# S5 recurrence of a hybrid diffusion step: sixteen lockstep chunk steps replaced by scan instructions on rotated states

## The chip, the cores and the metric

One core of a Trainium2 chip runs the whole program. The metric is the device time of one launch in microseconds, the median of the runs shown. Lower is better.

## The reference, cut to what matters

Two layers of a diffusion backbone work on 512 latent and 128 context tokens with 1024 channels. In each layer one projection feeds three mixers: a Hyena long convolution, a bidirectional S5 state space layer and a gated DeltaNet. The change lies in S5. It has 64 groups of 16 channels, each with 64 complex diagonal states per direction:

```python
lam_bar = jnp.exp(lam * step)
b_bar = ((lam_bar - 1.0) / lam)[..., None] * lax.complex(b_re, b_im)
bu = jnp.einsum('gph,blgh->blgp', b_bar, seq.astype(jnp.complex64))
bu = bu.at[:, 0].add(lam_bar * init)
_, xs = lax.associative_scan(_lin_combine, (a, bu), axis=1)   # x_t = lam_bar x_(t-1) + bu_t
finals.append(xs[:, -1])
yd = einsum('ghp,blgp->blgh', c_re, xs.real) - einsum('ghp,blgp->blgh', c_im, xs.imag)
```

It is run for both directions, for the latent tokens from cached states and for the context tokens from zero. The final context states are an output too.

## The kernel before

The residual stream lies transposed, channels on partitions and the 640 tokens along the free axis. Projections are products of split operands: a weight tile of 128x512 is loaded (`wr`), cast to `wh` on ACT (L69), its rest `wl` is formed on DVE or GpSimd (L70), and TensorE adds three products into `pj` or `pg` (L91). The order of the instructions on each engine isn't written by hand. The framework's scheduler makes it when the program is built, from the order in which the code is traced and from its own cost model; on the chip every engine then takes its instructions strictly in that order.

A layer has three parts: S5 and Hyena together, the DeltaNet, the merge. In the first, `run` takes turns between the generator `s5_core` and the generator `hyena`, one column tile (128 channels) each, eight times. The projections of the merge gates (`gates`, tile `pg`) are traced behind them and are drawn forward where TensorE would have nothing else. In layer 0 the modulation vectors (`mod_rest`, weights `in_wmod`, L286) are too.

For a column tile S5 works on 8 groups, with 64 states forward on the lower 64 partitions and 64 backward on the upper ones. The tokens are taken in 80 chunks of 8 (64 latent, 16 context):

- `s5_in` projects the tile, sends it through DRAM (`us`, then `U` with the 8 tokens of a chunk on partitions), builds the matrices `M2` on DVE and GpSimd (L824 to L829), and multiplies (L839): `X` holds what each chunk adds to the state. ACT moves it out of the accumulator (L841).
- `s5_scan` runs the recurrence over the chunks. The 80 chunks are five segments of 16, side by side. For each of 16 steps DVE does five small instructions (L884 to L888), and ACT copies the state that enters each chunk into `X`, once per direction (L895):

```python
nc.vector.tensor_tensor(out, z, bc(T["LR"]...), op=ALU.mult)
nc.vector.tensor_tensor(W, z[:, :, ::-1, :], bc(T["L2"]...), op=ALU.mult)
nc.vector.tensor_tensor(out, out, W, op=ALU.add)
for h, x in zip((lo, hi), add):
    nc.vector.tensor_tensor(out[h], out[h], x, op=ALU.add)
```

  Then the states that enter the later segments are chained (tile `C`) and their effect is added with the powers 0 to 15 of the chunk step, `FR` and `FI` (L912 to L916). GpSimd builds these powers by doubling in 24 small instructions (L865 to L871), and ACT adds a negated copy (L872).
- `s5_out` builds the read-out matrices `M3` (L949 to L954), the kernel of the convolution inside a chunk (`K`, through DRAM into `M1`), and multiplies (L981 to L983). In L981 and L982 the moving operand is `X[:, :, r, gi]`, whose neighbours along the chunks are 16 values apart.

`s5_core` traces `s5_in(i + 1)` and `s5_scan(i + 1)` ahead of `s5_out(i)`; `X` has two buffers.

Of the kernel before, what the change touches and what calls it, by code (L numbers as in the profile page):

```python
# [56 lines left out]
class Net:  # L57
# [242 lines left out]
    def mod_rest(self, l, p):  # L300
        """gate of layer l and all of layer l + 1"""
# [26 lines left out]
    def rstd_cols(self, p):  # L328
        """1/rms per token, tokens on partitions: [128, 5]"""
# [59 lines left out]
            # hidden layer of the filters: high parts above the low ones  # L389
# [12 lines left out]
    def hy_first(self, l, i, p):  # L402
        """channels 128 i .. 128 i + 127: spectra of the first order, factors of x1"""
# [10 lines left out]
    def hy_second(self, l, i, p, st):  # L414
        """spectra of the second order, factors of the output"""
# [11 lines left out]
    def hy_order1(self, l, i, p, st):  # L427
# [4 lines left out]
        # inverse, times x1, folded for the second order  # L432
# [78 lines left out]
    def filters(self, p, l, i, o, dec):  # L511
        """spectra (without the 1/norm) of order o for channel tile i"""
        nc, a, D, Dc = self.nc, self.a, self.D, self.Dc
        cs = slice(i * 128, i * 128 + 128)
        # forward + backward | forward - backward | forward columns, twice; high and low parts
# [19 lines left out]
        # even / odd parts of the two-sided filter, time tiles 0..127, 128..255 and their mirrors  # L535
# [3 lines left out]
        for t in range(2):  # L539
# [6 lines left out]
            # |fwd| + |bwd| = max(|fwd + bwd|, |fwd - bwd|)  # L546
# [59 lines left out]
        # slots 0: frequency 0 for Re, L for Im, each with half the weight of the others; even tile 1: L / 2  # L606
# [7 lines left out]
    def hy_in(self, p, l, t, rn, tag):  # L614
        """column tile -> conv -> folded, transposed: [time, 2, e | o, 128], context [time, 128]"""
# [229 lines left out]
    def s5_scan(self, l, ct, p, T):  # L845
# [44 lines left out]
        for s in range(16):  # L890
# [3 lines left out]
            for h, xv in zip((lo, hi), xs):  # L894
                nc.scalar.copy(xv, S[h])  # L895
# [768 lines left out]
```

## Time and profile before

| | |
|---|---|
| median of 3 runs | 3792.77 us (3789.83 to 3797.14) |
| span of the profiled execution | 3792.6 us |
| PE, PEld busy | 3401.0 us (90%), 3246.1 us (86%) |
| DVE, POOL, ACT busy | 2607.9 us (69%), 1692.8 us (45%), 1521.2 us (40%) |
| mean granted TensorE clock | 0.941 |

PE is TensorE's matmuls, PEld its weight loads, DVE VectorE, ACT ScalarE, POOL GpSimd. The profiled execution lies 0.2 us from the median, so its span stands for the time. The part of S5 and Hyena fills about 100 to 1000 us for layer 0 and 2000 to 2900 us for layer 1. The profile's chain of waits reaches back only to about 2979 us, behind both, so it says nothing on this part; the reading rests on the views that follow: stretches of time, waits, groups of instructions and single instructions.

### The profile page before, as it was taken

What the parts mean: (1) busy time and instruction counts of PE and PEld (TensorE: products, weight loads), DVE (VectorE), ACT (ScalarE), POOL (GpSimd) and SP (SyncE); (2) the same over time, 40 slices, a digit from 0 to 9 for tenths busy, and PEclk for the clock granted to TensorE, in tenths of its full rate; (3) what the DMA queues carried; (4) which work ended last, traced back from release to release, by engine and by line L of the source; (5) the groups of instructions that cost most, each with busy time, mean ns of one, the idle gap of its engine ahead of it and who ended that gap; (6) DMA issues with size and microseconds to landing.
All of it is one profiled execution on the core that took longest, in us unless ns stands there. A gap on an engine that the chain in (4) does not pass through costs nothing. (4 is left out here: it accounts for less than half of the span.)

```text
span 3792.6 us, 70255 instructions
## 1 busy us (share of the span) xinstructions
PE 3401.0 (90%) x25850; PEld 3246.1 (86%) x25850; DVE 2607.9 (69%) x6113; ACT 1521.2 (40%) x3519; POOL 1692.8 (45%) x2083
## 2 busy tenths in 40 slices
PE   6898988888989898899978899899899898798998
PEld 5788977788989888899977889898889898798998
DVE  6988788889237874643749788878883278776354
ACT  4533333333244555443334333333332445555422
POOL 4656555555344444301226565666654454351010
PEclk8899999999989999899989999999999899899999
DMA  6322233432231212543632222222222312224352
GB/s 226 113 75 67 75 94 103 119 97 58 79 86 63 71 60 71 175 141 111 197 104 77 73 65 73 75 81 72 72 61 73 96 63 78 61 92 140 126 176 89
DMA packets 310615, 362.89 MB, mean 96 GB/s; under 512 B 86814, under 2 KB 190270, under 8 KB 310016
## 3 DMA queue, kind: packets, MB, share of 16 engines
q1 hardware_dynamic: 305368, 357.75, 31.0%
q8 instruction: 204, 3.34, 0.4%
q10 hardware_dynamic: 4904, 0.66, 0.1%
q14 instruction: 139, 1.14, 0.1%
HBM read 291.74 MB, written 66.54 MB: 94 GB/s over the span
## 5 line engine op out<-in xcount | busy, mean ns | idle before, releaser
L91 PE MATMUL pj<-hh,wh 128*128 128x320 f32 x2048 | 670.7, 328 | 77.5 <-ACT wh L69 32.4
L91 PE MATMUL pj<-hl,wh 128*128 128x320 f32 x2048 | 662.0, 323 | 2.4 <-DVE hl L70 2.4
L91 PE MATMUL pj<-hh,wl 128*128 128x320 f32 x2048 | 660.0, 324 | 2.8 <-POOL wl L70 1.5
L69 ACT CAST wh<-wr 128x512 fp32r<-128x512 f32 x608 | 375.0, 618 | 598.4 <-PE pj L91 396.9
L70 POOL TENSOR_TENSOR wl<-wr,wh 128x512 fp32r<-128x512 f32 x288 | 382.4, 1331 | 517.0 <-ACT wh L69 466.9
L91 PEld LDWEIGHTS pj<-hh,wh 128*128 128x128 f32 x2048 | 404.3, 197 | 89.7 <-ACT wh L69 33.7
L91 PE MATMUL pg<-hh,wh 128*128 128x320 f32 x1280 | 416.6, 326 | 14.1 <-ACT wh L69 10.2
L91 PE MATMUL pg<-hl,wh 128*128 128x320 f32 x1280 | 412.8, 323 | 0.0
L70 DVE TENSOR_TENSOR wl<-wr,wh 128x512 fp32r<-128x512 f32 x320 | 244.1, 764 | 244.5 <-ACT wh L69 242.1
L91 PE MATMUL pg<-hh,wl 128*128 128x320 f32 x1280 | 409.9, 324 | 1.6 <-POOL wl L70 1.6
L91 PEld LDWEIGHTS pj<-hl,wh 128*128 128x128 f32 x2048 | 403.2, 197 | 6.5 <-DVE hl L70 5.3
L91 PEld LDWEIGHTS pj<-hh,wl 128*128 128x128 f32 x2048 | 402.4, 197 | 5.9 <-POOL wl L70 2.8
L91 PE MATMUL pj<-yh,wh 128*128 128x320 f32 x1024 | 316.8, 311 | 3.6 <-ACT yh L69 2.4
L91 PE MATMUL pj<-yl,wh 128*128 128x320 f32 x1024 | 317.4, 311 | 2.4 <-DVE yl L70 2.3
L91 PE MATMUL pj<-yh,wl 128*128 128x320 f32 x1024 | 316.4, 310 | 0.0
L895 ACT COPY X<-Z 64x80 f32<-64x80 f32 x512 | 131.1, 256 | 386.7 <-DVE Z L888 380.1
L91 PEld LDWEIGHTS pg<-hh,wh 128*128 128x128 f32 x1280 | 252.1, 197 | 18.9 <-ACT wh L69 11.3
L91 PEld LDWEIGHTS pg<-hh,wl 128*128 128x128 f32 x1280 | 249.1, 196 | 4.1 <-POOL wl L70 2.7
L91 PEld LDWEIGHTS pg<-hl,wh 128*128 128x128 f32 x1280 | 251.7, 197 | 0.7 <-issue 0.4
L888 DVE TENSOR_TENSOR Z<-Z,X 64x80 f32<-64x80 f32 x512 | 209.0, 408 | 13.7 <-ACT X L841 1.1
L91 PEld LDWEIGHTS pj<-yh,wh 128*128 128x128 f32 x1024 | 192.5, 189 | 4.9 <-ACT yh L69 3.2
L91 PEld LDWEIGHTS pj<-yl,wh 128*128 128x128 f32 x1024 | 192.8, 188 | 4.2 <-DVE yl L70 4.2
(513 smaller groups left out, 8757.1 us busy)
## 6 DMA issues: line engine op xcount, KB each, us to landing
wr<-in_wt SPq DMA_DIRECT2D x608, 256.0 KB, 2.7
gt<-gst SPq DMA_DIRECT2D x160, 160.0 KB, 2.0
gt<-gt SPq DMA_DIRECT2D x64, 320.0 KB, 3.3
wr<-in_wmod SPq DMA_DIRECT2D x64, 256.0 KB, 3.1
Pm<-gcd SPq DMA_DIRECT2D x32, 320.0 KB, 11.2
wm<-in_wmod SPq DMA_DIRECT2D x4, 2048.0 KB, 18.6
M<-ks SPq DMA_DIRECT2D x256, 32.0 KB, 1.8
xd<-x SPq DMA_DIRECT2D x16, 320.0 KB, 4.3
```

The lines of the kernel that those rows point to most:

```text
L69: self.nc.scalar.copy(h, src)
L70: (eng or self.nc.vector).tensor_tensor(l, src, h.bitcast(F32), op=ALU.subtract)
L91: ins = self.nc.tensor.matmul(o, w[:, k, :m], x[:, kh * 4 + k, s], start=kh == 0 and k == 0 and i == 0, stop=kh == 1 and k == 3 and i == 2)
L888: nc.vector.tensor_tensor(out[h], out[h], x, op=ALU.add)
L895: nc.scalar.copy(xv, S[h])
```

## The change

The step of a state over one chunk is a complex number of length `r8` and angle `theta`. Chunk states are turned back by their own angle (multiplied by e to the minus i theta c, with c the chunk's place), so that the recurrence has the real factor `r8`; then one scan instruction per real or imaginary part and direction does the whole recurrence, and the states are turned forward again. The columns of a group are now 83: 64 latent, 16 context, and places for entering states and a zero factor in `A` that stops the recurrence between segments and groups. The powers of the rotation, `E`, are built for each column tile on GpSimd by seven doublings, each of which takes its factor from two small ACT instructions. `E` and `A` have one buffer, `R` and `X` too; `X` now has its chunks side by side in memory. `s5_core` traces `s5_scan(i)`, then `s5_in(i + 1)`, then `s5_out(i)`. `s5_tables` computes the tables for this instead of those for the segments. The removed code is that of the kernel above.

```diff
@@ s5_core
+        E = cp.tile([128, 2, 8, 83], F32, name="E")
+        nc.gpsimd.memset(E[:, 0, :, 0:1], 1.0)
+        nc.gpsimd.memset(E[:, 1, :, 0:1], 0.0)
+        A = cp.tile([128, 8, 83], F32, name="A")
+        nc.gpsimd.memset(A, 0.0)
         self.s5_in(l, 0, p, T)
-        st = self.s5_scan(l, 0, p, T)
         for i in range(8):
-            now = st
+            now = self.s5_scan(l, i, p, T)
             if i < 7:
                 self.s5_in(l, i + 1, p, T)
-                st = self.s5_scan(l, i + 1, p, T)
             self.s5_out(l, i, p, T, *now)
+    def s5_turns(self, ct, p, T):
+        nc, E, A = self.nc, T["E"], T["A"]
+        gq = slice(8 * ct, 8 * ct + 8)
+        nc.scalar.copy(E[:, :, :, 1], T["V"][:, :, gq])
+        for x, n in ((slice(1, 65), 64), (slice(66, 82), 16)):
+            nc.scalar.copy(A[:, :, x], bc(T["r8"][:, gq].unsqueeze(2), [128, 8, n]))
+        e = 1
+        while e < 82:
+            n = min(e, 82 - e)
+            s, d = slice(1, 1 + n), slice(e + 1, e + 1 + n)
+            sh = [128, 2, 8, n]
+            m = p.tile([128, 2, 8, 1], F32, name="em", bufs=2)
+            nc.scalar.mul(m[:, 0], E[:, 1, :, e:e + 1], -1.0)
+            nc.scalar.copy(m[:, 1], E[:, 1, :, e:e + 1])
+            t = p.tile([128, 2, 8, 32], F32, name="et", tag="W5")[:, :, :, 0:n]
+            nc.gpsimd.tensor_tensor(E[:, 0:2, :, d], E[:, 0:2, :, s], bc(E[:, 0:1, :, e:e + 1], sh), op=ALU.mult)
+            nc.gpsimd.tensor_tensor(t, E[:, ::-1, :, s], bc(m, sh), op=ALU.mult)
+            nc.gpsimd.tensor_tensor(E[:, 0:2, :, d], E[:, 0:2, :, d], t, op=ALU.add)
+            e *= 2
@@ s5_in
-            nc.scalar.mul(T2[i][hi], src[hi, 0:8, gq], sg)
+        g.tensor_tensor(T2[hi, 0], pr, vr, op=ALU.mult)
...
-                nc.scalar.copy(X[:, :, r, ls].rearrange("p j g -> p g j"),
-                               pi.rearrange("p (g c) -> p g c", g=4)[:, :, 0:80])
+                nc.scalar.copy(R[:, r, ls, 1:83], pi.rearrange("p (g c) -> p g c", g=4)[:, :, 0:82])
+        nc.scalar.copy(R[:, :, :, 0:66:65], T["si"][:, :, gq, :])
@@ s5_scan
+        self.s5_turns(ct, p, T)
+        X = p.tile([128, 2, H, 83], F32, name="X5")
+        W = p.tile([128, H, 83], F32, name="W5")
+        re, im = E[:, 0], E[:, 1]
+        def turn(z, sg):
+            for r in range(2):
+                nc.vector.tensor_tensor(X[:, r], z[:, r], re, op=ALU.mult)
+                nc.vector.tensor_tensor(W, z[:, 1 - r], im, op=ALU.mult)
+                nc.vector.tensor_tensor(X[:, r], X[:, r], W, op=ALU.add if (r == 0) == (sg < 0) else ALU.subtract)
+        turn(R, -1)
+        for r in range(2):
+            z, b = [y[:, r].rearrange("p g c -> p (g c)") for y in (R, X)]
+            nc.vector.tensor_tensor_scan(z[lo], af[lo], b[lo], 0.0, op0=ALU.mult, op1=ALU.add)
+            nc.vector.tensor_tensor_scan(z[hi, n - 3::-1], af[hi, n - 1:1:-1], b[hi, n - 1:1:-1], 0.0,
+                                         op0=ALU.mult, op1=ALU.add)
+        turn(R, 1)
+        for h, s in ((lo, 81), (hi, 64)):
+            for r in range(2):
+                nc.scalar.mul(fs[h, :, r], X[h, r, :, s], -1.0 if r else 1.0)
@@ s5_out
-                nc.tensor.matmul(o, M3[:, 0, g, 1:9, :], X[:, :, 0, gi], start=True, stop=False)
+                nc.tensor.matmul(o, M3[:, 0, g, 1:9, :], X[:, 0, gi, 0:82], start=True, stop=False)
...
-            nc.scalar.copy(y[:, 320 * st:320 * st + 320], py[:, :320])
+            nc.scalar.copy(v[:, :, 0:64], o[:, :, 0:64])
+            nc.scalar.copy(v[:, :, 64:80], o[:, :, 65:81])
```

The scheduler makes a new order of the whole program. Three pieces of it, each from a column tile in the middle of layer 0, show what the prediction speaks of. The numbers behind the names are buffers; the brackets name the engines whose work an instruction waits for. First, DVE's queue before, in the middle of the recurrence. L667, L668 and L635 belong to Hyena.

```order
L886 TENSOR_TENSOR Z_4922<-Z_4922,W_4923 128x80 [waits DVE_49]
L888 TENSOR_TENSOR Z_4922<-Z_4922,X_4795 64x80 [waits DVE_49]
L888 TENSOR_TENSOR Z_4922<-Z_4922,X_4795 64x80
L667 TENSOR_TENSOR p1_5507<-pb_5498,KP_4471 128x512 [waits PE_49]
L884 TENSOR_TENSOR Z_4931<-Z_4922,LR_597 128x80 [waits DVE_49,Activation_49]
L885 TENSOR_TENSOR W_4932<-Z_4922,L2_633 128x80
L635 TENSOR_TENSOR hytx_5493<-pb_5486,rn_4506 128x512 [waits PE_49]
L668 TENSOR_TENSOR p2_5508<-pb_5498,KE_4472 128x512 [waits Pool_49]
```

Hyena's instructions stand one by one between the steps of the recurrence. Now DVE's queue of the changed kernel where the first turn of a column tile begins; `W5<-R5,E` is its first instruction.

```order
L138 TENSOR_SCALAR mod1_96<-mod1_96,ng1_93 128x2 [waits DVE_49] x2
L930 TENSOR_TENSOR W5_5164<-R5_4265,E_681 128x664 [waits Activation_49,Pool_49]
L124 SCALAR_TENSOR_TENSOR hyy_4727<-pj_4666,hcw_1259,hyy_4727 128x127 [waits DVE_49]
L1002 TENSOR_TENSOR K_4365<-K_4365,pb_4366 128x16 [waits DMAHW3_49,PE_49,Activation_49]
L132 SCALAR_TENSOR_TENSOR K_4365<-c128_66,sd_677,K_4365 128x16 [waits DVE_49]
L635 TENSOR_TENSOR hytx_4743<-pb_4736,rn_3894 128x512 [waits PE_49]
L636 TENSOR_TENSOR hycx_4744<-pb_4737,rn_3894 128x128 [waits PE_49]
L667 TENSOR_TENSOR p1_4757<-pb_4748,KP_3859 128x512 [waits PE_49]
```

That instruction waits for POOL's last power and for ACT, and behind it stand Hyena's `hyy`, `hytx`, `p1` and S5's `K`. Counted in the order, the turns and scans of this tile lie in a stretch of 73 rows of DVE, 16 of them their own; 52 rows lie between the last reader of `E` of one tile and the first of the next. The first instruction that writes `X` stands 45 rows after `W5<-R5,E`, 18 rows behind the second `K` of the tile before, and waits for that tile's read-out on TensorE. Last, POOL's queue of the changed kernel while it builds the powers of a tile (`E`, `et`); `am` and `w3s` are Hyena's.

```order
L831 TENSOR_TENSOR E_681<-E_681,et_5124 128x16x2 [waits Pool_49]
L829 TENSOR_TENSOR E_681<-E_681 128x16x4 [waits Pool_49]
L830 TENSOR_TENSOR et_5131<-E_681,em_5128 128x16x4 [waits Activation_49]
L831 TENSOR_TENSOR E_681<-E_681,et_5131 128x16x4 [waits Pool_49]
L554 TENSOR_TENSOR am_4497<-ab_4504 128x128 [waits DVE_49]
L829 TENSOR_TENSOR E_681<-E_681 128x16x8 [waits Pool_49]
L521 TENSOR_TENSOR w3s_5507<-w3r_5502 128x128 [waits DVE_49]
L522 TENSOR_TENSOR w3s_5507<-w3r_5502 128x128
L830 TENSOR_TENSOR et_5138<-E_681,em_5135 128x16x8 [waits Activation_49]
```

Each round's second instruction waits for ACT's `em`, and the next `em` on ACT waits for the round's last instruction here. Counted in the order, the 21 instructions of a tile's powers lie in a stretch of 46 rows of POOL; the other 25 are Hyena's and S5's.

## Rows read from the trace of the kernel before

**Rows 1.** Windows in us: PE, PEld, DVE, ACT, POOL busy (count); clock; DMA; GB/s.

```profile
100.00:1000.00 900.00, 800.86 (x6163) 745.37 (x6163) 744.12 (x1752) 324.74 (x874) 516.00 (x711) 0.94 0.30 87
2000.00:2900.00 900.00, 817.48 (x5958) 780.99 (x5957) 730.84 (x1685) 328.32 (x884) 528.02 (x713) 0.95 0.26 72
900.00:1000.00 100.00, 94.01 (x697) 88.85 (x697) 61.28 (x126) 24.11 (x58) 46.92 (x50) 0.98 0.30 73
2100.00:2200.00 100.00, 94.18 (x652) 91.17 (x651) 70.33 (x160) 34.45 (x85) 56.60 (x78) 0.95 0.25 74
2800.00:2900.00 100.00, 93.45 (x690) 89.32 (x690) 66.49 (x143) 25.48 (x66) 49.01 (x54) 0.95 0.30 75
```

**Rows 2.** Waits of PE, 110 to 990 us: total, times, longest.

```profile
PE pb L965 <- DVE T L936: 16.1, 5, 4.4
PE pg L286 <- DMA wr<-in_wmod: 11.6, 9, 2.1
PE pb L983 <- DMA M<-ks: 6.2, 6, 1.6
...
PE pb L530 <- DVE KE L596: 0.3, 1, 0.3
```

**Rows 3.** Instructions of one line of Hyena, layer 0: min/median/max ns, first, last start.

```profile
L477 DVE TENSOR_TENSOR v<-pb,yo x8: 410/424/427, 273.3 to 1000.8; 128x256 f32<-128x256 f32 x8
```

**Rows 4.** Groups by form, DVE: count, total us, mean ns, idle before them and releaser.

```profile
L888 DVE TENSOR_TENSOR Z<-Z,X 64x80 f32<-64x80 f32 x512 | 209.0, 408 | 13.7 <-ACT X L841 1.1
L886 DVE TENSOR_TENSOR Z<-Z,W 128x80 f32<-128x80 f32 x256 | 95.4, 373 | 4.4
L884 DVE TENSOR_TENSOR Z<-Z,LR 128x80 f32<-128x80 f32 x256 | 88.2, 345 | 12.7 <-ACT X L895 0.9
L885 DVE TENSOR_TENSOR W<-Z,L 128x80 f32<-128x80 f32 x256 | 78.5, 306 | 0.1
L916 DVE TENSOR_TENSOR X<-X,D 64x256 f32<-64x256 f32 x96 | 57.7, 602 | 1.4
L914 DVE TENSOR_TENSOR D<-D,E 128x256 f32<-128x256 f32 x48 | 28.7, 598 | 0.1
```

**Rows 5.** Instructions of one line: S5's add of two products of 128x640.

```profile
L951 DVE TENSOR_TENSOR M<-M,m3t x32: 805/1234/2175, 165.6 to 2847.7; 128x640 f32<-128x640 f32 x32
```

**Rows 6.** Groups by form, DVE, nearest to a scan: a fused pair, a slow operation.

```profile
L411 DVE RECIPROCAL rn<-rn 128x256 f32<-128x256 f32 x16 | 27.9, 1745 | 4.4 <-POOL rn L136 4.3
L120 DVE SCALAR_TENSOR_TENSOR hyy<-pj,hcw,hyy 128x511 f32<-128x511 f32 x32 | 23.8, 743 | 5.8 <-ACT hyy L115 5.0
```

**Rows 7.** Instructions in order of time, PE: start, us to the last end, count.

```profile
573.04 0.46 PE L981 MATMUL pb<-X,M 128*128 128x80 f32 x2
573.33 0.45 PE L982 MATMUL pb<-X,M 128*128 128x80 f32 x2
573.60 0.36 PE L983 MATMUL pb<-U,M 128*128 128x80 f32 x2
573.80 0.46 PE L981 MATMUL pb<-X,M 128*128 128x80 f32 x2
```

**Rows 8.** Groups by form, POOL: powers of before (dearest, cheapest), larger products.

```profile
L866 POOL TENSOR_TENSOR ft<-FI,LI 128x8 f32<-128x8 f32 x16 | 6.2, 385 | 7.1 <-DVE FI L858 7.1
L869 POOL TENSOR_TENSOR FI<-FR,LI 128x16 f32<-128x16 f32 x16 | 3.5, 216 | 0.0
L669 POOL TENSOR_TENSOR Y<-p,p 128x256 f32<-128x256 f32 x64 | 55.4, 866 | 164.1 <-DVE p L668 146.3 <-DVE FI L858 11.0 <-DMA scr<-in_scr 5.9
L597 POOL TENSOR_TENSOR KP<-KE,c 128x512 f32<-128x512 f32 x32 | 44.6, 1393 | 32.6 <-DVE KE L596 9.6 <-DVE Z L888 7.8 <-DVE Z L886 5.1
```

**Rows 9.** Groups by form, ACT.

```profile
L895 ACT COPY X<-Z 64x80 f32<-64x80 f32 x512 | 131.1, 256 | 386.7 <-DVE Z L888 380.1
L872 ACT ACTIVATE FI<-FI 128x128 f32<-128x128 f32 x16 | 5.0, 310 | 41.9 <-POOL FI L871 41.8
L904 ACT COPY C<-Z 64x16 f32<-64x16 f32 x16 | 3.2, 200 | 0.0
```

More of the change, by code (lines that the diff above doesn't have):

```diff
@@ L694, in s5_tables @@
             nc.scalar.dma_start(st[64 * d:64 * d + 64, :], bc(a["ls"][l, d:d + 1, :], [64, G]))
+        s0 = p.tile([128, 2, G], F32, name="s0")
+        nc.scalar.dma_start(s0, a["s0"][l].rearrange("p (c g) -> p c g", c=2))
         nc.gpsimd.tensor_tensor(st, self.ebase[:, 0:G], st, op=ALU.pow)
@@ L715, in s5_tables @@
                       PR[:, s, :], PI_[:, s, :], sh, "pw%d" % n)
-        LR = cp.tile([128, 5, G], F32, name="LR")
-        LI = cp.tile([128, 5, G], F32, name="LI")
-        nc.vector.tensor_copy(LR[:, 0, :], PR[:, 8, :])
-        nc.vector.tensor_copy(LI[:, 0, :], PI_[:, 8, :])
-        for n in range(4):
-            re, im = LR[:, n, :], LI[:, n, :]
-            self.cmul(nc.vector, p, LR[:, n + 1, :], LI[:, n + 1, :], re, im, re, im, [128, G], "lsq")
-        L2 = cp.tile([128, 2, 2, G], F32, name="L2")
-        nc.vector.tensor_copy(L2[:, :, 0, :], LI[:, 0:5:4, :])
-        self.ts(nc.vector, L2[:, :, 1, :], LI[:, 0:5:4, :], -1.0)
+        for n in range(3):
+            re, im = CS[:, n, 0, :], CS[:, n, 1, :]
+            self.cmul(nc.vector, p, CS[:, n + 1, 0, :], CS[:, n + 1, 1, :], re, im, re, im, [128, G], "lsq")
+        c8 = CS[:, 3]
+        q = p.tile([128, 2, G], F32, name="lq")
+        nc.vector.tensor_tensor(q, c8, c8, op=ALU.mult)
+        nc.vector.tensor_tensor(q[:, 0, :], q[:, 0, :], q[:, 1, :], op=ALU.add)
+        self.ts(nc.vector, q[:, 0, :], q[:, 0, :], -0.5, 1.5)
+        nc.vector.tensor_tensor(c8, c8, bc(q[:, 0:1, :], [128, 2, G]), op=ALU.mult)
+        r8 = cp.tile([128, G], F32, name="r8")
+        nc.vector.tensor_tensor(r8, mag, mag, op=ALU.mult)
+        for n in range(2):
+            nc.vector.tensor_tensor(r8, r8, r8, op=ALU.mult)
+        V = cp.tile([128, 2, G], F32, name="V5")
+        nc.vector.tensor_copy(V[:, 0, :], c8[:, 0, :])
+        for x, sg in ((lo, -1.0), (hi, 1.0)):
+            self.ts(nc.vector, V[x, 1, :], c8[x, 1, :], sg)
+        v2 = cp.tile([128, 2, G], F32, name="lv2")
+        vr, vi = v2[hi, 0], v2[hi, 1]
+        x = p.tile([128, 2, G], F32, name="lv3")
+        nc.vector.tensor_tensor(x[hi], V[hi, 0:2], V[hi, 0:2], op=ALU.mult)
+        nc.vector.tensor_tensor(vr, x[hi, 0], x[hi, 1], op=ALU.subtract)
+        self.stt(vi, V[hi, 0], 2.0, V[hi, 1])
+        si = cp.tile([128, 2, G, 2], F32, name="si")
+        nc.vector.memset(si, 0.0)
+        self.ts(nc.vector, s0[:, 1, :], s0[:, 1, :], -1.0)
+        nc.vector.tensor_copy(si[lo, :, :, 0], s0[lo])
+        self.cmul_hi(p, si[hi, 0, :, 1], si[hi, 1, :, 1], s0[hi, 0, :], s0[hi, 1, :], vr, vi)
         m2 = p.tile([128, G], F32, name="lm2")
@@ L780, in s5_in @@
         Pu = self.proj(l, W_S5 + ct, self.hh, self.hl, T["q"])
-        u = p.tile([128, 8, 80], F32, name="u")
-        nc.scalar.copy(u, Pu.rearrange("p (j t) -> p t j", t=8))
+        u = p.tile([128, 8, 82], F32, name="u", tag="ys")
+        nc.gpsimd.memset(u[:, :, 64:82:17], 0.0)
+        nc.scalar.copy(u[:, :, 0:64], Pu[:, 0:NLAT].rearrange("p (j t) -> p t j", t=8))
+        nc.scalar.copy(u[:, :, 65:81], Pu[:, NLAT:].rearrange("p (j t) -> p t j", t=8))
         nc.sync.dma_start(T["us"][ct * 128:(ct + 1) * 128], u)
@@ L819, in s5_in @@
             m2v = M2.rearrange("p r g (t h) -> p r g t h", t=8)
-            tv = [bc(x.rearrange("p t g -> p g t")[:, ls, :].unsqueeze(3), sh) for x in T2]
+            tv = [bc(T2[:, i, :, ls].rearrange("p t g -> p g t").unsqueeze(3), sh) for i in range(2)]
             bv = [bc(x[:, ls, :].unsqueeze(2), sh) for x in (BR, BI)]
@@ L872, in s5_scan @@
-        nc.scalar.mul(FI[:, :, 1, :], FI[:, :, 0, :], -1.0)
-        S = p.tile([128, 5, 2, H], F32, name="Z", bufs=3)
-        nc.vector.memset(S, 0.0)
-        nc.scalar.copy(S[lo, 0], T["s0"][lo, :, gq])
-        nc.scalar.copy(S[hi, 3], T["s0"][hi, :, gq])
-        sh = [128, 5, 2, H]
-        def step(out, z, n, sh, add):
-            W = p.tile([128, 5, 2, H], F32, name="W", bufs=2)[:, :sh[1]]
-            nc.vector.tensor_tensor(out, z, bc(T["LR"][:, n:n + 1, gq].unsqueeze(1), sh), op=ALU.mult)
-            nc.vector.tensor_tensor(W, z[:, :, ::-1, :], bc(T["L2"][:, n // 4:n // 4 + 1, :, gq], sh), op=ALU.mult)
-            nc.vector.tensor_tensor(out, out, W, op=ALU.add)
-            for h, x in zip((lo, hi), add):
-                nc.vector.tensor_tensor(out[h], out[h], x, op=ALU.add)
@@ L890, in s5_scan @@
-        for s in range(16):
-            xs = (X[lo, s:80:16], X[hi, 15 - s:80:16])
-            Sn = p.tile([128, 5, 2, H], F32, name="Z", bufs=3)
-            step(Sn, S, 0, sh, xs)
-            for h, xv in zip((lo, hi), xs):
-                nc.scalar.copy(xv, S[h])
-            S = Sn
+        self.s5_turns(ct, p, T)
[7 more added lines that the diff above has]
+                nc.vector.tensor_tensor(X[:, r], X[:, r], W, op=ALU.add if (r == 0) == (sg < 0) else ALU.subtract)
```

112 lines of the change are left out of this document (47 added, 65 removed).

## The prediction

> **What bounds the kernel now.** I read first the busy time by stretches, since the change touches only the part where S5 and Hyena run together. In its two stretches of 900 us PE is busy for 800.86 and 817.48 us, 89.0% and 90.8%, at a granted clock of 0.94 and 0.95; DVE for 744.12 and 730.84, 82% together; POOL for 57% [rows 1]. So TensorE is the bound in name, with a tenth of the part idle, and DVE stands close behind it. Three stretches of 100 us show what PE does when DVE has less to do: at 61.28, 70.33 and 66.49% DVE, PE reaches 94.01, 94.18 and 93.45%, 93.9% in the mean [rows 1]. This is what the reader is to see there: PE's idle tenth goes with DVE's load.
>
> The waits of PE say the same. From 110 to 990 us 18 rows of PE's waits end with DVE, from 16.1 us down to 0.3 us, 51 us in all; the largest other one is a DMA, the modulation weights of layer 0, with 11.6 us [rows 2]. TensorE takes its instructions in a fixed order, so each late product of DVE stops the whole queue, filler and all. The pace is 103.9 us for a column tile: Hyena's L477 runs eight times from 273.3 to 1000.8 us, seven intervals [rows 3].
>
> **DVE.** For each of 16 column tiles (8 in each of 2 layers) the change removes the recurrence. The six groups shown sum to 557.5 us, 34.8 us for a tile [rows 4]; the chain of segment states and L912 and L913, twins of L914, are left out of the sum. It adds twelve turns and four scans, all of 664 elements. A turn multiplies or adds two operands of SBUF, as S5's L951 does, which took 805 to 2175 ns for 640 elements, 1234 in the median [rows 5]: 1.28 us for 664, 0.84 to 2.26 as bounds, so 15.4 us for a tile (10.0 to 27.1). No row shows a scan. It does two operations per element, as L120 does in 743 ns for 511, 0.97 us for 664; the slowest row per element, a reciprocal of 256 in 1745 ns, would make it 4.5 us [rows 6]. I take the fused pair, whose kind of work it is nearest to: 3.9 us for a tile (3.3, at L951's fastest rate, to 18.1). Together 19.3 us (13.3 to 45.2) against 34.8: DVE is relieved by 15.5 us for a tile (from 21.5 to a loss of 10.4). At 82% of 103.9 us it had 85 us of work; it is left with about 70, 67%, which is inside the three stretches above.
>
> [...]
>
> **TensorE.** The products with `X` start 0.29 and 0.27 us before the next one, the same product with `U` 0.20 us (573.33, 573.60 and 573.80 less the starts ahead of them) [rows 7]. The only difference in the code is that neighbours of `X` lie 16 values apart, and now they lie side by side. So each pair becomes cheaper by 0.16 us; there are 4 groups, 2 halves, 16 tiles, 128 pairs: 20.5 us, and nothing if the stride is not the cause. 82 columns in place of 80 or 96 I cost at nothing.
>
> **GpSimd.** The powers of before are 24 instructions of 385 to 216 ns, about 0.30, 7.2 us for a tile. The new ones are 21: nine of 16 to 64 elements at 0.30; three of 128 at about 0.55, between this and the 866 ns of 256; three of 256 at 0.87, three of 288 at 0.94, three of 512 at 1.39 [rows 8]: 14.0 us. The turned `T2` adds six small ones, 2 us. POOL gains 9 us for a tile, 57% become 66%. Its cover is its own idle time; without it the loop below decides.
>
> [...]
>
> **ACT.** 32 copies of 256 ns go, 8.2 us for a tile, and so does the lockstep: ACT sat idle for 380.1 us in the two layers until DVE had a state for it [rows 9]. In come 14 factors for the doublings and some other small pieces at 0.20 us [rows 9], 4 us. The copies out of the accumulators change form and stay about even. ACT is busy for 36% of the part, which covers it.
>
> **The moved waits.** DMAs stay the same in number and place, apart from the states' output, which is written off any path. Two waits are new on DVE. The first turn waits for the powers and has Hyena's instructions behind it, and the next writes `X`, which now has one buffer, so it waits for the read-out of the tile before. In the order that write stands 18 rows behind the second `K`, some 8 us of DVE's work at the mean row below, in which `K` goes through DRAM into `M1` and the read-out runs. TensorE itself waited for that trip six times in layer 0, 1.6 us at most [rows 2]. I cost it at nothing under these 8 us; without them it is up to 1.6 us for a tile, 26 us in all. The former closes a loop: `E` is free after the last turn, is rebuilt on POOL and ACT, and lets the next turns begin. DVE's share: 19.3 us of turns and scans and 57 other rows at the part's mean of 0.42 us (744.12 over 1752), 24 us; at the 82% at which it ran, 53 us. POOL's share: 14.0 us and 25 other rows at 0.73 (516.00 over 711), 32 us. With seven handoffs between POOL and ACT of h each the loop takes 85 + 7h. ACT needs 0.4 us for a factor, and POOL works meanwhile on the round's first product, 0.3 to 1.4 us; with ACT's queue I take 1.5 us for h, 95.5 us in all, under the pace.
>
> **The sum.** PE's 1618.3 us of work in both stretches less 20.5 are 1597.8; at 93.9% busy they take 1702 us in place of 1800: 98 us less. I give back 12 us, since the modulation weights of layer 0 are waited for as before, and 1 us for each tile (16 us), since the handoffs now stand in ACT's queue ahead of the copies that TensorE waits for. 70 us remain: 3792.6, the profiled execution's span, becomes 3722. The median of the runs shown is 3792.77, so nothing is to be added. At the layers' heads the first powers wait for nothing of S5 and are covered by its first projection.
>
> **Rivals.**
> - *More than that.* DVE is what holds the rest too, and PE runs at 97%: 1597.8 / 0.97 is 1647, 153 us less, 3640. For it: the 51 us of waits in one layer are half of the idle time, and ACT's lockstep goes as well. Against it: no stretch of this part shows over 94.2%.
> - *The loop takes DVE's place.* h is what L872 waited for POOL, 41.8 us in 16 cases, 2.6 us [rows 9]: 85 + 18 = 103 us, the pace of before. Then the relief is eaten by the wait for the powers and only TensorE's 20 us are left, or less: 3772 to 3795. For it: the powers are asked for as soon as they are ready in the order, without slack. [...]
> - *Slower.* The same loop past 2.7 us a handoff, the point from which it is longer than 103.9. At 3.5 it takes 109.5 us, 5.6 more in 14 intervals, 78 us: 3871 at the worst, about 3830 if half of it is hidden by filler. ACT's queue would do this: before an `em` stand copies that wait for TensorE. Against it: the first product of a round hides part of every handoff.
> - *Nothing there.* The scans cost 4.5 us each and turns 2.3, DVE loses 10.4 us a tile: its 85 us become 95, and the kernel stays near 3790. This needs every bound at its worst.
>
> **Chances.** The forecast, 3690 to 3760: 0.55. More than that: 0.15. The loop in DVE's place or nothing there: 0.15. Slower: 0.15. Counted as the same is what lies within 0.2%, 7.6 us, about what a measurement of this kernel can tell from no change. Of the third case about half lies there, a part of it is still faster: faster 0.77, same 0.07, slower 0.16. The range takes in most of the first three cases and the near end of the slower one: 3645 to 3800.
>
> **What would show it.** Right: DVE near 67% and PE at 93% or more in the part, PE's waits for DVE halved, X products 0.20 us apart, a pace near 98 us. Wrong: DVE's first turn waiting long for POOL or ACT, rows of ACT idle until POOL's last instruction of a round, POOL over 70%; scans far over 1.5 us; or waits of PE that only change their names.

## The result and the profile after

The changed kernel takes 3731.73 us (median of 4 runs, 3730.83 to 3732.30). The kernel before, run on the same chip, takes 3794.95 (4 runs, 3789.83 to 3799.97). The ratio is 0.9834, with a 95% interval of 0.982 to 0.9848: 63 us less. The forecast was 3722, the range 3645 to 3800. The profiled execution after has a span of 3730.3 us and stands for the time.

The busy time of each engine, whole program, after:

```profile
PE 3380.0 (91%) x25850; PEld 3220.4 (86%) x25850; DVE 2369.6 (64%) x4615; ACT 1413.4 (38%) x3295; POOL 1942.9 (52%) x2153
```

PE is busy for 21 us less (from 3401.0) and idle for 41 us less (391.6 to 350.3, the spans less the busy times). DVE has lost 238 us, ACT 108, and POOL has gained 250. The mean granted TensorE clock is 0.950 (0.941 before).

Two stretches of 900 us inside the part of S5 and Hyena, which now ends earlier in layer 1 (columns as in [rows 1]):

```profile
100.00:1000.00 900.00, 824.35 (x6397) 768.91 (x6397) 625.26 (x1006) 279.81 (x777) 654.23 (x763) 0.96 0.33 89
1950.00:2850.00 900.00, 839.02 (x6267) 799.23 (x6266) 626.74 (x951) 292.39 (x792) 665.24 (x759) 0.98 0.30 78
```

PE is busy for 92.4% of them in the mean (89.9% in [rows 1]), DVE for 70%, and POOL for 73%: GpSimd is now ahead of VectorE. Below are PE's longest waits in each of the two layers; the first fence is 110 to 990 us, as [rows 2], the second 1950 to 2850 us.

```profile
PE pb L908 <- DMA U<-us: 12.0, 4, 4.7
PE pj L91 <- DVE wl L70: 7.8, 3, 3.5
```

```profile
PE pb L468 <- POOL Y L670: 9.4, 4, 2.7
PE pb L468 <- POOL Y L669: 8.0, 4, 3.1
```

Summed over all rows of that view by the engine waited for, in us, layer 0 and layer 1 (the same two stretches in both kernels):

| PE waited for | before | after |
|---|---|---|
| DVE | 51.3, 51.9 | 18.3, 5.7 |
| POOL | 7.2, 5.4 | 15.1, 27.7 |
| ACT | 19.7, 26.6 | 17.0, 18.6 |
| DMA | 18.0, 7.4 | 22.6, 7.2 |

The waits for DVE are nearly gone. A third of what they were has come back under POOL's name, above all at Hyena's products `Y`.

What DVE does in the new recurrence, groups by form (count, total us, mean ns, idle before them and releaser):

```profile
L930 DVE TENSOR_TENSOR W<-R,E 128x664 f32<-128x664 f32 x64 | 68.7, 1073 | 2.9 <-ACT R L911 1.8 <-POOL E L831 0.8
L931 DVE TENSOR_TENSOR X<-X,W 128x664 f32<-128x664 f32 x64 | 65.6, 1025 | 0.3
L929 DVE TENSOR_TENSOR X<-R,E 128x664 f32<-128x664 f32 x64 | 64.1, 1019 | 10.1 <-PE pb L1014 6.5 <-ACT R L911 3.2
L939 DVE TENSOR_TENSOR_SCAN R<-A,X 64x662 f32<-64x662 f32 x32 | 58.5, 1828 | 0.4
L938 DVE TENSOR_TENSOR_SCAN R<-A,X 64x664 f32<-64x664 f32 x32 | 53.9, 1685 | 0.1
...
L981 DVE TENSOR_TENSOR M<-T,scr 128x640 f32<-128x640 f32 x32 | 34.4, 1075 | 51.1 <-PE pb L1014 43.5 <-PE pb L129 7.5
```

The turns cost 198.4 us, 12.4 for a tile, the scans 112.4, 7.0 for a tile. The wait for the powers, on which two rivals rested, is 0.8 us in 64 cases. DVE now idles where the next `M3` waits for the read-out of the one before, 43.5 us in all; what that costs no run shows.

The read-out on TensorE, which [rows 7] shows with the strided `X`:

```profile
L1015 PE MATMUL pb<-U,M 128*128 128x82 f32 x256 | 51.7, 285 | 12.3 <-DMA gt<-gst 4.6 <-DMA wr<-in_wt 3.4 <-DMA M<-ks 3.0
L1014 PE MATMUL pb<-X,M 128*128 128x82 f32 x256 | 51.5, 284 | 0.0
L1013 PE MATMUL pb<-X,M 128*128 128x82 f32 x256 | 50.3, 279 | 1.5 <-DVE K L1002 1.5
```

The three products now cost the same. The same groups before:

```profile
L981 PE MATMUL pb<-X,M 128*128 128x80 f32 x256 | 61.6, 330 | 17.3 <-DVE K L970 14.7 <-DVE X L916 2.2
L982 PE MATMUL pb<-X,M 128*128 128x80 f32 x256 | 60.0, 324 | 0.0
L983 PE MATMUL pb<-U,M 128*128 128x80 f32 x256 | 49.6, 276 | 14.7 <-DMA M<-ks 12.1 <-DMA sbr<-in_sbr 1.5 <-issue 1.1
```

Each product is two of these records, and records overlap: before, a product with two records of 330 ns in the mean started 0.29 us ahead of the next [rows 7]. So such a mean is not what a product adds to the queue. The busy times of the three groups sum to 171.2 us before and 153.5 after, 17.7 less. The starts, in order of time, show less still. After:

```profile
560.84 0.39 PE L1013 MATMUL pb<-X,M 128*128 128x82 f32 x2
561.07 0.39 PE L1014 MATMUL pb<-X,M 128*128 128x82 f32 x2
561.29 0.39 PE L1015 MATMUL pb<-U,M 128*128 128x82 f32 x2
561.51 0.39 PE L1013 MATMUL pb<-X,M 128*128 128x82 f32 x2
```

From one `L1013` to the next it is 0.67 us; before, the same three took 0.76 (573.80 less 573.04) [rows 7]. The product with `U`, which started its successor after 0.20 us, now takes 0.22 like the others.

POOL's powers, all sizes together, and ACT's factor for them:

```profile
L830 POOL TENSOR_TENSOR et<-E,em 128x16 f32<-128x16 f32 (+6 forms) x112 | 77.6, 693 | 5.3 <-ACT em L827 5.0
L831 POOL TENSOR_TENSOR E<-E,et 128x16 f32<-128x16 f32 (+6 forms) x112 | 77.3, 691 | 3.5
L829 POOL TENSOR_TENSOR E<-E 128x16 f32<-128x16 f32 (+6 forms) x112 | 73.2, 654 | 19.4 <-ACT E L816 15.7
```

```profile
L826 ACT ACTIVATE em<-E 128x8 f32<-128x8 f32 x112 | 24.1, 215 | 143.2 <-POOL E L831 142.5
```

They are 228 us, 14.3 for a tile. POOL waits for ACT's factors for 5.0 us in all. ACT, in turn, stands 142.5 us until POOL is ready. Other work of POOL became slower too:

```profile
L669 POOL TENSOR_TENSOR Y<-p,p 128x256 f32<-128x256 f32 x64 | 86.3, 1349 | 124.9 <-DVE p L668 119.4 <-DVE K L1002 5.0
...
L843 POOL MEMSET u<- 128x16 f32 x16 | 2.0, 126 | 49.1 <-DMA gd<-ys 46.3 <-DMA us<-u 2.5
```

`Y` took 866 ns in the mean for the same tile before [rows 8]. The second row is a wait that nobody had forecast: the memset of `u` stands until the stores of `y` have left the buffer that they share.

Where the time went, by place: Hyena's L477 of each layer, with the columns of [rows 3], and the merge gates' products `pg` that lie between its first and last start (stretch, its length, PE busy and count), of the kernel before and of the changed one.

```profile
L477 DVE TENSOR_TENSOR v<-pb,yo x8: 409/411/425, 271.4 to 988.6; 128x256 f32<-128x256 f32 x8
L477 DVE TENSOR_TENSOR v<-pb,yo x8: 409/416/425, 2139.4 to 2854.3; 128x256 f32<-128x256 f32 x8
```

```profile
273.30:1000.80 727.50, 121.94 (x1053) 0.95 0.31 87
2171.30:2908.50 737.20, 153.62 (x895) 0.95 0.26 72
```

```profile
271.40:988.60 717.20, 135.98 (x1127) 0.95 0.33 90
2139.40:2854.30 714.90, 162.19 (x951) 0.97 0.28 75
```

The pace is 717.2 / 7 = 102.5 us in layer 0, hardly less than the 103.9 of [rows 3], and 102.1 in layer 1 (105.3 before). But the new order puts more filler into the same stretch, 14.0 and 8.6 us of it. Without that the intervals would be 100.5 and 100.9 us. The filler is then missing behind the part, so the gain shows there. The layer's last product with `yh` ends the merge and is free of this; in layer 0 it starts at

```profile
L91 PE MATMUL pj<-yh,wh x512: 305/309/416, 1638.4 to 1871.4; 128*128 128x320 f32 x171
```

before and, after, at

```profile
L91 PE MATMUL pj<-yh,wh x512: 302/309/636, 1597.4 to 1847.1; 128*128 128x320 f32 x171
```

Layer 0 is shorter by 24.3 us up to there, and the rest of the program by 38.0.

### The profile page after: what moved, and what is told of

Same layout as the page of the kernel before. It is cut to its first block, busy times and chain, and to the rows that moved or that the text cites. A ratio compares the mean times of both kernels' runs of the same rounds, so it can differ in the third digit from the quotient of the medians.

```text
span 3730.3 us, 68509 instructions
## 1 busy us (share of the span) xinstructions
PE 3380.0 (91%) x25850; PEld 3220.4 (86%) x25850; DVE 2369.6 (64%) x4615; ACT 1413.4 (38%) x3295; POOL 1942.9 (52%) x2153
## 5 line engine op out<-in xcount | busy, mean ns | idle before, releaser
L70 POOL TENSOR_TENSOR wl<-wr,wh 128x512 fp32r<-128x512 f32 x288 | 392.1, 1365 | 448.9 <-ACT wh L69 388.7
L70 DVE TENSOR_TENSOR wl<-wr,wh 128x512 fp32r<-128x512 f32 x320 | 259.5, 812 | 244.4 <-ACT wh L69 243.1
L91 PEld LDWEIGHTS pj<-hh,wl 128*128 128x128 f32 x2048 | 398.8, 195 | 14.9 <-DVE wl L70 9.3
L91 PEld LDWEIGHTS pg<-hh,wh 128*128 128x128 f32 x1280 | 250.4, 196 | 19.4 <-ACT wh L69 11.6
L91 PEld LDWEIGHTS pg<-hh,wl 128*128 128x128 f32 x1280 | 247.4, 194 | 14.2 <-POOL wl L70 12.5
L91 PEld LDWEIGHTS pj<-yh,wl 128*128 128x128 f32 x1024 | 193.6, 189 | 0.0
L1514 POOL TENSOR_TENSOR m<-m,gt 128x640 f32<-128x640 f32 x16 | 31.1, 1943 | 295.8 <-DVE gt L132 295.8
```

Of the source, the lines that this page charges most:

```text
L70: (eng or self.nc.vector).tensor_tensor(l, src, h.bitcast(F32), op=ALU.subtract)
L91: ins = self.nc.tensor.matmul(o, w[:, k, :m], x[:, kh * 4 + k, s], start=kh == 0 and k == 0 and i == 0, stop=kh == 1 and k == 3 and i == 2)
L1514: nc.gpsimd.tensor_tensor(m[i], m[i], g, op=ALU.add)
```

## Experiments

Each ratio is to the kernel before, run beside it. To set kernels of different batches against the changed kernel, its ratio of 0.9834 is taken off and the difference multiplied by 3795 us (last column).

| run | median us | ratio, 95% interval | against the changed kernel |
|---|---|---|---|
| before_side | 3838.85 | 1.0104, 1.0085 to 1.0123 | (before: +39) |
| after_apart | 3783.14 | 0.9956, 0.9939 to 0.9973 | +46 |
| turn_twice | 3746.55 | 0.9882, 0.9858 to 0.9905 | +18 |
| turn_thrice | 3811.91 | 1.0029, 1.0017 to 1.0041 | +74 |
| powers_once | 3688.09 | 0.9705, 0.9685 to 0.9725 | -49 |
| powers_twice | 3811.04 | 1.0046, 1.0028 to 1.0063 | +80 |
| powers_no_act | 3748.02 | 0.986, 0.9843 to 0.9876 | +10 |
| powers_dve | 3760.16 | 0.9899, 0.9884 to 0.9913 | +25 |
| powers_split | 3730.63 | 0.9833, 0.9812 to 0.9853 | 0 |
| zeros_on_act | 3734.10 | 0.9823, 0.9808 to 0.9838 | -4 |
| no_act_zeros | 3747.45 | 0.9859, 0.9845 to 0.9874 | +10 |
| bi_first | 3739.03 | 0.9857, 0.9833 to 0.988 | +9 |

**How much an order alone does: bi_first.** Only the order in which six GpSimd instructions are written is changed: the three that make `BI` stand ahead of the three that make `BR`. The scheduler moves a good part of every queue.

> The same work as in the changed kernel: only the six GpSimd instructions for BR and BI are written in the other order. The scheduler answers with another order of the whole program (some half of PE's rows stand elsewhere). This measures how far an order alone moves the time. If differences of 10 to 15 us between the variants are effects of their edits, this kernel lies within 8 us of the changed one, 3724 to 3740. If they are what another order does, it lies more than 8 us away on either side.

It is 9 us slower by the ratios, 7 by the medians, with an interval that overlaps the changed kernel's. So another order can move the time by some 9 us with the same work, and no difference of that size below is put down to an edit. PE's busy time moves as well: the same matmuls fill 3367.5 us here and 3380.0 in the changed kernel.

**DVE's load: turn_twice and turn_thrice.** The last turn, done again with the same result.

```diff
-        turn(R, 1)
+        for _ in range(3):
+            turn(R, 1)
```

> The changed kernel with the last turn of each column tile done three times over, with the same result each time: 12 more instructions of about 1.04 us on DVE for a tile, 200 us in all, which gives DVE nearly the load back that the change took from it (238 us by the two profiles). Theory A (PE's idle time went down since DVE has less to do): DVE near 2570 us busy, PE's waits for DVE come back, and 30 to 45 us of the gain are lost, 3762 to 3777 us. Rival (the gain beside the stride comes from the new order or from ACT's freed queue, and DVE's load is hidden): within 8 us of 3732.

> The last turn is done twice: six instructions of 1.05 us more on DVE for a tile, some 95 us in all, and the same result. If DVE's load is priced evenly, half of what the third turn cost as well: 80 / 2, so 3765 to 3780. If the load costs only past a point (over 75% of the part): under 15 us, 3732 to 3747.

DVE's work grew by 80 us with the second turn and by 183 with the third (2449.7 and 2552.5 us against 2369.6), the time by 18 and 74. The first 80 us cost 0.2 us each, the next 103 us over 0.5. So neither expectation has the size: 74 us is more than the 30 to 45 of turn_thrice, and 18 lies between the two cases of turn_twice. Load on DVE costs time, and in these two runs more the less room is left. Over the two stretches PE's waits for DVE come back from 24 us to 51 with the third turn, and those for POOL rise from 43 to 63. The third turn in layer 0 (110 to 990 us) shows where it bites, in DVE's waits:

```profile
DVE p L667 <- POOL Y L670: 47.2, 22, 6.3
```

Hyena's `p` and `Y` go back and forth between DVE and POOL; the same row of the changed kernel reads

```profile
DVE p L667 <- POOL Y L670: 26.6, 20, 2.2
```

**The stride: before_side and after_apart.** The first gives the kernel before an `X` with chunks side by side, so that DVE's and ACT's small instructions take the stride and TensorE doesn't. The second gives the changed kernel an `X` whose chunks lie 16 values apart, written so by the last turn.

```diff
-        X = p.tile([128, 80, 2, H], F32, name="X", bufs=2)
+        X = p.tile([128, 2, H, 80], F32, name="X", bufs=2)
```

> The kernel before with the chunks of X side by side in memory (X as part, group, chunk in place of chunk, part, group), nothing else. Theory A (the stride of the moving operand makes the two products with X dear): they start 0.20 us apart like the product with U, PE is busy some 20 us less, and the kernel comes out near 3775 us. Rival (the stride is not the cause, the products with X are dear for another reason, or the time is not PE's): no change, within 8 us of 3795, PE busy as before.

```diff
-        turn(R, 1)
+        turn(R, 1, XV)      # XV = XF.rearrange("p (c r g) -> p r g c", r=2, g=H)
```

> The changed kernel with the last turn written so that neighbouring chunks of X lie 16 values apart again, as before the change. Theory A: the products with X go back to 0.28 us, PE's busy time rises by some 20 us, and the kernel loses about 20 us, 3752 us. Rival: no change, 3732 us within 8 us; or the turn that writes with the stride becomes dearer on DVE, which its row would show.

The rows of the two products move both ways as expected; PE's busy time as a whole does not. It is 3413.0 us in before_side (12 more than before, 20 less were expected) and 3390.1 in after_apart (10 more, 20 were expected). In groups by form, the products of before_side, and its recurrence on DVE:

```profile
L982 PE MATMUL pb<-X,M 128*128 128x80 f32 x256 | 53.3, 293 | 0.0
L981 PE MATMUL pb<-X,M 128*128 128x80 f32 x256 | 53.2, 292 | 20.4 <-DVE K L970 16.6 <-DVE X L916 3.8
```

```profile
L888 DVE TENSOR_TENSOR Z<-Z,X 64x80 f32<-64x80 f32 x512 | 240.8, 470 | 13.1 <-ACT X L841 0.5
...
L916 DVE TENSOR_TENSOR X<-X,D 64x256 f32<-64x256 f32 x96 | 75.3, 784 | 1.4
```

and the products and the last turn's share in after_apart:

```profile
L1015 PE MATMUL pb<-X,M 128*128 128x82 f32 x256 | 60.6, 326 | 1.9 <-DVE K L1004 1.9
L1016 PE MATMUL pb<-X,M 128*128 128x82 f32 x256 | 60.0, 323 | 0.0
```

```profile
L931 DVE TENSOR_TENSOR X<-R,E 128x664 f32<-128x664 f32 x64 | 80.8, 1278 | 25.1 <-PE pb L1016 22.6 <-ACT R L911 2.3
L933 DVE TENSOR_TENSOR X<-X,W 128x664 f32<-128x664 f32 x64 | 78.8, 1232 | 0.2
```

The products with `X` fall from 330 and 324 ns to 293 and 292 in the one and rise from 279 and 284 to 326 and 323 in the other. So the stride is what makes them dear. The product with `U`, whose operand did not change, goes the other way: from 276 to 289 ns and from 285 to 272. Yet before_side is slower: L888 rises from 408 to 470 ns and L916 from 602 to 784 [rows 4], 50 us in all on the engine that PE waits for. In after_apart DVE carries 46 us more. Neither run isolates what the stride on TensorE costs in time, because in both DVE's work grew too. They show that without the scans the layout that suits TensorE is a loss, and that with them it is worth 46 us. The three groups of products account for 16 of it (169.2 us busy in after_apart, 153.5 in the changed kernel); that the rest comes from DVE's 46 us is likely, but not shown apart.

**What the powers cost: powers_once and powers_twice.** In the first `E` and `A` are built for the first column tile of a layer only, so seven of eight tiles take the first one's powers; the second builds them twice.

```diff
-        self.s5_turns(ct, p, T)
+        if ct == 0:
+            self.s5_turns(ct, p, T)
```

> The changed kernel with the powers of the rotation and the scan's factors built for the first column tile of a layer only; those of the other seven tiles are left out and the first tile's are used in their place. 14 of 16 builds go: some 14 us of GpSimd and 21 small pieces of ACT for each. Theory A (the forecast took the build to be covered but for about 1 us of TensorE's waits for a tile): 10 to 20 us faster, 3712 to 3722. Rival (the build on GpSimd and its handoffs hold the part back, so that most of what DVE gave was eaten): 35 us faster or more, under 3697. If GpSimd's idle time covers all of it: 3732 within 8 us.

> The powers of each column tile are built twice, the second time over the first: 336 more instructions on GpSimd, 228 us by the rows of the changed kernel, and 224 factors on ACT. If the build's cost of 44 us is its load (0.2 to 0.25 us of span for 1 us of GpSimd's work): 3775 to 3800. If the build costs by a loop that ends last (E free, rebuilt, next turns), a second build of some 20 us for each tile lies on it in full: 3900 or more. If the 44 us were an effect of another order alone: 3725 to 3750.

Without the build the kernel is 49 us faster, as in the rival and not the 10 to 20 us of theory A; with two builds it is 80 us slower, past the range for load and far below that for the loop. POOL's busy time moves by -180 and +169 us (1762.5 and 2112.2 against 1942.9). So the build costs as load, and more as POOL fills: 0.27 us for each us taken off, 0.47 for each added. Not all of it need be POOL's own: without the build DVE's busy time falls by 40 us too (2329.6 against 2369.6), for the same instructions. In powers_twice POOL is busy for 81 and 80% of the two stretches:

```profile
100.00:1000.00 900.00, 796.52 (x6178) 739.97 (x6178) 620.86 (x959) 292.12 (x884) 731.57 (x914) 0.96 0.34 89
1950.00:2850.00 900.00, 811.57 (x5892) 768.65 (x5893) 583.52 (x870) 312.63 (x909) 721.65 (x907) 0.96 0.30 78
```

The loop from the last turn over the build to the next turn is not what costs: the first turns, which need the finished powers, still find them nearly ready.

```profile
L931 DVE TENSOR_TENSOR W<-R,E 128x664 f32<-128x664 f32 x64 | 70.7, 1104 | 3.9 <-POOL E L832 3.6
L930 DVE TENSOR_TENSOR X<-R,E 128x664 f32<-128x664 f32 x64 | 65.1, 1034 | 26.2 <-PE pb L1015 23.2 <-POOL E L832 2.4 <-ACT R L912 0.4
```

**Handoffs or work: powers_no_act, zeros_on_act, no_act_zeros.** The doubling without ACT's factor, the zero columns of `u` written by ACT in place of POOL's waiting memset, and both.

```diff
-            nc.gpsimd.tensor_tensor(t, E[:, ::-1, :, s], bc(m, sh), op=ALU.mult)
-            nc.gpsimd.tensor_tensor(E[:, 0:2, :, d], E[:, 0:2, :, d], t, op=ALU.add)
+            nc.gpsimd.tensor_tensor(t, E[:, ::-1, :, s], bc(E[:, 1:2, :, e:e + 1], sh), op=ALU.mult)
+            nc.gpsimd.tensor_tensor(E[:, 0, :, d], E[:, 0, :, d], t[:, 0], op=ALU.subtract)
+            nc.gpsimd.tensor_tensor(E[:, 1, :, d], E[:, 1, :, d], t[:, 1], op=ALU.add)
```

> The doubling is done on GpSimd alone: the imaginary factor is read from E itself, and the last add of a round becomes a subtraction for the real half and an addition for the imaginary half. So ACT's 14 factors for a tile (em, 45.4 us busy and the 142.5 us for which ACT stands before them until POOL's last instruction of a round) are gone, and with them seven exchanges between the two engines; POOL gets seven more small instructions for a tile (112 in all, at 0.3 us some 34 us). Theory H (the 44 us that the build of the powers costs come from the handoffs, which hold ACT's copies back behind them): 3690 to 3715. Theory P (they come from the work itself, on POOL and in contention with DVE): no gain, 3725 to 3745.

```diff
-        nc.gpsimd.memset(u[:, :, 64:82:17], 0.0)
+        nc.scalar.copy(u[:, :, 64:82:17], bc(T["A"][:, 0:1, 0:1], [128, 8, 2]))
```

> The two zero columns of u are written by ACT (a copy of zeros) in place of GpSimd's memset, which stood 46.3 us in all until the stores of y had left the buffer that u shares. ACT's next instructions wait for the same buffer anyway. Theory P (POOL's queue is late at Hyena's products Y, for which PE waits 28 us in layer 1): 46 us of stall go from POOL's queue, at 0.24 some 11 us, up to 25: 3707 to 3722. Theory H (POOL's load has room, only the handoffs cost): no difference, 3727 to 3737.

> Both edits together, the doubling on GpSimd alone and the zero columns on ACT. If the two act on different waits their differences add: theory H 3690 to 3715, theory P 3710 to 3735.

Without any handoff to ACT the kernel gains nothing (+10 alone, +10 with the zeros on ACT as well, about what an order does). So ACT's 142.5 us of standing cost nothing that shows. Nor does POOL's wait of 46 us at the memset: without it the time is the same. So theory H falls, and of theory P the part that put the cost on that stall.

**Which engine: powers_dve and powers_split.** The same doubling on VectorE, without ACT's factors, all of it or its first four rounds.

```diff
-            nc.gpsimd.tensor_tensor(E[:, 0:2, :, d], ...)
+            nc.vector.tensor_tensor(E[:, 0:2, :, d], ...)
```

> The same doubling without ACT's factors, all of it on VectorE: 28 instructions for a tile that touch some 3900 elements, at DVE's rates of the changed kernel's turns (1.0 to 1.6 ns per element, with 0.1 us each for the start) 7 to 9 us for a tile, 110 to 145 us in all; POOL loses 228 us. If an engine that is about twice as fast on such work settles it: 3690 to 3715. If DVE's load is what PE's idle time goes with (0.44 us of span for 1 us of DVE's work by the run with the turn done three times, 0.24 for 1 us of POOL's by the run with the powers built once): plus 50 to 65 and less 55, so 3725 to 3745.

> The first four rounds of the doubling (up to 8 powers for each of 16 rows, 32 to 256 elements an instruction) are done on VectorE, the last three on GpSimd, none with ACT's factors. On VectorE the sixteen small instructions for a tile take some 0.2 us, 3 us for a tile, 50 us in all; GpSimd loses 12 instructions of 0.3 to 0.7 us, some 5 us for a tile, 85 us, and wins the three additional ones of the large rounds. By the slopes of 0.44 and 0.24: plus 22 less 15, no gain, 3730 to 3750. If small instructions belong on the engine with the cheaper start and the wait of a round for the next is what costs: 3700 to 3720.

All on VectorE is 25 us slower, though POOL loses 190 us and DVE gains only 142. Neither expectation holds. The slopes measured above, 0.27 for POOL and 0.2 to 0.5 for DVE, would have made it about even, so slopes of two engines can't simply be added. PE's waits for DVE rise from 24 to 59 us over the two stretches. The large instructions are faster on VectorE: 512 elements take 0.9 us against 1.25 to 1.31 on GpSimd in the changed kernel, which is 1.4 times as long and not about twice, as 1393 ns [rows 8] are to the 743 for 511 elements [rows 6] (groups by form of powers_dve):

```profile
L827 DVE TENSOR_TENSOR et<-E 128x16 f32<-128x16 f32 x16 | 15.6, 977 | 0.0
L827 DVE TENSOR_TENSOR et<-E 128x512 f32<-128x512 f32 x16 | 15.1, 942 | 0.0
L826 DVE TENSOR_TENSOR E<-E 128x512 f32<-128x512 f32 x16 | 14.0, 875 | 0.3
L829 DVE TENSOR_TENSOR E<-E,et 128x16 f32<-128x16 f32 x16 | 2.7, 166 | 0.0
```

Small ones vary: of two groups of 16 elements one takes 977 ns in the mean, as long as 512 elements, and the other 166. What holds the first up is not shown. In all, the 28 instructions for a tile take 223 us on VectorE, where 110 to 145 were expected, and 259 on GpSimd (powers_no_act). The split is even with the changed kernel. No complete version that was run beats it by more than another order does.

## Why the prediction was right, and where it was not

**The sum.** 70 us less were forecast and 63 came. PE's idle time fell by 41 us, where 98 less 20.5 less 28, about 49, were forecast. That the sum comes so near is in part luck: its terms miss in both directions.

**DVE, right in the sum by errors that cancel.** The relief was put at 15.5 us for a tile; DVE's busy time fell by 238.3 / 16 = 14.9. The new work was put at 19.3 us and is 19.4. But a turn was taken at 1.28 us, from L951, and takes 1.02 to 1.07; a scan was taken at 0.97, from the fused pair of L120, and takes 1.69 to 1.83. The step that failed is "I take the fused pair, whose kind of work it is nearest to": 2.5 to 2.8 ns for an element against 1.45. The relief has two more errors that cancel. The groups left out of the sum (L912, L913 and the chain in tile `C`) took 105.2 us, so the recurrence was 41.4 us for a tile and not 34.8, and the relief by rows is 22. But DVE's busy time did not fall by that much: other instructions on it became longer, the one that makes the weights' rest `wl` (L70) from 244.1 to 259.5 us, and its records overlap less: all its groups sum to 2861.5 us before, in 2607.9 us busy, and to 2554.9 after, in 2369.6. The scans took 1.7 to 1.9 times the 0.97 us of the fused pair.

**PE follows DVE, right in direction.** PE's waits for DVE fell to a quarter (103.2 to 24.0 us in both layers), and turn_thrice takes back more than the whole gain, though DVE's load stays below that of before (2552.5 against 2607.9 us). So DVE's load is not all that holds PE. The step that was too good is the 93.9%, read from stretches in which DVE had less to do and POOL was at 47 to 57%. PE reached 92.4%, with POOL at 73%. Two other stretches of before, which the prediction passes over, show PE nearly as high with DVE as busy as ever (columns as in [rows 1]):

```profile
2200.00:2300.00 100.00, 92.89 (x678) 88.66 (x677) 82.47 (x203) 36.49 (x105) 58.33 (x91) 0.95 0.28 80
2300.00:2400.00 100.00, 92.16 (x668) 87.55 (x667) 87.41 (x203) 37.14 (x100) 60.13 (x84) 0.93 0.24 64
```

PE's idle time went with DVE's load less closely than the three stretches said.

**TensorE's stride: the cause right, the size too large.** 20.5 us were forecast and 21.0 came off PE's busy time, but that is chance, since bi_first moves this time by 12.5 us with the same matmuls. The three groups lost 17.7 us of busy time, and by the starts shown it is 0.76 less 0.67 in 128 cases, 11.5 us. The step that failed takes the 0.20 us of the product with `U` as the price without a stride: all three products take 0.22 to 0.23. after_apart and before_side show the cause both ways.

**POOL, the step that failed most.** "POOL gains 9 us for a tile, 57% become 66%. Its cover is its own idle time; without it the loop below decides." (Over both stretches the 57% are 58.) The powers were sized well (14.0 us forecast, 14.3 measured), `T2` too (2.2 against 2). But POOL gained 250 / 16 = 15.6 us for a tile, since its other instructions became longer: `Y` by 483 ns in 64 cases, 31 us, the largest of them. The build isn't what lengthens `Y`, since it takes 1362 ns in powers_once too. Nor is it the amount of DVE's turns, as min/median/max ns of the changed kernel and of turn_thrice show:

```profile
L669 POOL TENSOR_TENSOR Y<-p,p x96: 449/766/4284, 211.8 to 2847.8; 128x256 f32<-128x256 f32 x64, 128x128 f32<-128x128 f32 x32
L669 POOL TENSOR_TENSOR Y<-p,p x96: 447/736/1447, 208.7 to 2948.1; 128x256 f32<-128x256 f32 x64, 128x128 f32<-128x128 f32 x32
```

The median hardly differs; a few cases are very long, and with the turns done three times they are gone, while the kernel is 74 us slower. In the changed kernel 24 of the 30 that last over 1150 ns run beside a turn or scan of DVE; the other 34 of 128x256, which last 0.72 to 0.74 us, run beside none. Whether that lengthens them was not tried apart. And POOL's idle time did not cover the build: powers_once shows 44 (medians) to 49 us (ratios) that the build takes, where the sum gave back 16. The build takes them as load, not through the loop and not by the handoffs.

**The loop and the handoffs, harmless as forecast, for another reason.** The handoff was put at 1.5 us; POOL waited for ACT's factor 5.0 us in 112 cases. The two rivals that rest on it did not come: the first turn waits 0.8 us for POOL. The handoffs in ACT's queue, for which the 16 us were given back, cost nothing that can be measured.

**The rest.** The write of `X` waits 6.5 us for the read-out in all, forecast as nothing. PE's waits for the modulation weights halved (5.5 us), though 12 us had been kept for them. The pace, put near 98 us, is 102; it was no fair sign, since the order decides how much filler lies between two tiles. The rival in which PE runs at 97% is refuted, and "nothing there" too.

**What stays open.** Which waits add up to the build's 49 us. PE's waits sum to 132 us in the changed kernel and to 138 in powers_once, over both stretches, so no wait of PE's carries it; PE's busy time is 33 us less there (3346.9), spread over nearly all its groups by some 3 us at most each, at a granted clock of 0.954. But PE's busy time is no safe measure: in no_act_zeros it is 24 us less (3356.1), at 0.955, and that kernel is 10 us slower. Whether the clock makes the difference, or matmuls that wait in a way that the profile counts as busy, the runs don't tell. The new order in which `s5_core` traces its pieces, the single buffers of `R` and `X`, and ACT's 108 us less were not tried apart from the scans either.

## What to carry to other kernels

Where one engine waits for a second, moving the second's work to a third is worth what the third leaves over: here the kernel gained 63 us, and without the build on GpSimd (powers_once) it gains some 45 to 50 more. So cost the moved work on the receiving engine as time, by a slope from a run with the work done twice, and not as hidden by its idle share. Measure a move between two engines itself: the two slopes did not add up to what powers_dve cost. Look for waits only after that: 142 us and 46 us of standing in two queues were worth nothing here.

## What the runs showed of the hardware

- A record of a matmul of 82 columns in four-byte values lasts 279 to 285 ns when the moving operand's columns lie side by side and 323 to 326 when they lie 64 bytes apart (after against after_apart). From start to start a product of two such records takes 0.22 to 0.23 us with columns side by side; with 80 columns 64 bytes apart it took 0.27 to 0.29 [rows 7].
- A scan of 662 or 664 elements on 64 partitions takes 1.69 to 1.83 us in the mean, 2.5 to 2.8 ns for an element.
- GpSimd's add of 128x256 (`Y`) took 866 ns in the mean in the kernel before, 1349 in the changed one and 1362 in powers_once, the same instruction on the same tile; of all sizes of it the longest case took 4284 ns in the changed kernel and 1447 in turn_thrice. On VectorE (powers_dve) two groups of 16 elements took 977 and 166 ns in the mean.
- For the powers, 512 elements in one instruction took 0.88 and 0.94 us on VectorE (powers_dve) and 1.25 and 1.31 us on GpSimd (the changed kernel), 1.4 times as long. With all of this work on VectorE the kernel is 25 us slower than the changed one.
- The rows of the three pieces of order ran in the order in which they stand: DVE before from 532.81 to 535.69 us, DVE of the changed kernel from 531.30 to 535.90, and POOL from 496.80 to 501.22.
